# First projection groups of a hybrid decoder step on raw x: the norm's factor and the shift applied to the sums

## The chip, the cores and the metric

The kernel runs on one core of one Trainium2 chip. The time is the device time of one execution in microseconds (us); three executions before the change took 2463.82, 2465.86 and 2465.92, median 2465.86.

The core's engines run side by side, each through its own list of instructions in order: PE multiplies matrices (PEld is its loading of weights), DVE (VectorE), ACT (ScalarE) and POOL (GpSimd) work element by element, SP issues the DMAs here. An instruction waits for the engines whose results or buffers it needs; everything behind it on the same engine waits with it.

## The reference

One decoder layer on 1024 prompt tokens and 8 x 8 sample tokens. What matters here is its start:

```python
mod = jax.nn.silu(c) @ ada_w + ada_b
shift, scale, gate = jnp.split(mod, 3, axis=-1)
h = _rmsnorm(x, norm_g) * (1.0 + scale[:, None]) + shift[:, None]
proj = h @ w_in
```

with `_rmsnorm(x, g) = x * rsqrt(mean(x*x) + EPS) * g`. The prompt has one vector c, each of the 8 sample sequences its own, so that scale and shift have nine columns. The projection's parts then go through windowed attention, a gated MLP and a matrix memory, and an output projection; none of that is touched by the change.

## The kernel before

**Layout.** x is held transposed: 16 tiles (k = 0 to 15) of 128 features by 1088 tokens (1024 of the prompt, 64 samples), worked on in chunks of 384, 384 and 320 tokens (`CH`, line 25). Everything is float32. For the products each value is split into a high part, rounded to the fast matmul format, and a low part, the rest; three matmuls (high by high, high by low, low by high: `products`, lines 249 to 254) make one product. So every tile of the normed and modulated x becomes hH[k] and hL[k], and every weight block becomes wh (rounded by ACT, line 98) and wl (subtracted by POOL, line 99). SP loads the blocks ahead of time into four buffers, and four split blocks exist at a time.

**The start (lines 300 to 595).** In this order:
- SP loads the constants, c, all 16 tiles of x (line 312), then the modulation's weights in pieces of 0.5 MB (lines 326 and 329), four buffers ("ad") at a time, and the first weight blocks.
- As each tile lands, ACT or DVE squares it (lines 387, 389), and PE adds up the squares over the features with a matmul by ones (`token_sums`, line 272). After the sixteenth, `token_rsqrt` (lines 275 to 297) turns the sums, takes the root with three steps of Newton on DVE, and lets PE and ACT spread the result over all partitions: rbc, the norm's factor of each token.
- Tiles are multiplied by rbc (`scaled`, line 398): 0 and 1 by DVE, the others by POOL.
- The modulation comes in groups of two tiles. `ada_half` (tiles 0 and 1, four pieces each) and `ada_group` (two tiles, eight pieces) multiply silu(c) by the pieces in four sets, ACT copies the sums, PE turns them (line 374), DVE reduces them and adds the constants (lines 376, 409 to 411). Then DVE multiplies and shifts the tile (line 420; lines 423 and 424 for the samples), ACT rounds it to hH (line 425), DVE (for four tiles POOL) subtracts to hL (line 431).
- Four column tiles (the v part of the gated MLP) are accumulated meanwhile in four SBUF accumulators acc0 to acc3: for each group g of two tiles there are 12 units (four columns by three chunks) of six matmuls in one of four PSUM buffers, and DVE adds each to its accumulator (line 584). Group 0 is run as two single tiles (lines 542 to 570), groups 1 to 7 in the loop at 574. The table `AT` says after which unit of a group which step of a later modulation group is issued: that hand-written order is the order in each engine's list.
- `gate_column` (lines 625 to 636) follows as the first stage that needs all 16 hH and hL; then come the other columns, which keep PE busy to the end of the kernel.

hH, hL, x and the squares share 33 buffers of one tile each ("slots", line 123).

Of the kernel before, what the change touches and what calls it, by code (L numbers as in the profile page):

```python
# [20 lines left out]
NB = 8  # L21
# [52 lines left out]
class Weights:  # L74
# [16 lines left out]
    def split_to(self, j):  # L91
        while self.ns <= min(j, len(self.jobs) - 1):
            self.dma_to(self.ns)
            n = self.jobs[self.ns][1] * 128
            raw = self.raw.pop(self.ns)
            wh = self.pool.tile([128, 512], FR, tag="wh", name="wh", bufs=4)
            wl = self.pool.tile([128, 512], FR, tag="wl", name="wl", bufs=4)
            self.nc.scalar.copy(wh[:, :n], raw[:, :n])  # L98
            self.nc.gpsimd.tensor_tensor(wl[:, :n], raw[:, :n], wh[:, :n].bitcast(FT), op=OP.subtract)  # L99
            self.parts[self.ns] = (wh, wl)  # L100
            self.ns += 1
# [10 lines left out]
def body(tc, I, O):  # L112
# [162 lines left out]
    def token_rsqrt(ps, n, out, wait):  # L275
# [3 lines left out]
        S.copy(t[64:96, :320], ps[64:96, :320])  # L279
# [23 lines left out]
    ctt = et("ctt")[:, :KT * ND9].rearrange("p (k r) -> p k r", k=KT)  # L303
    SP.dma_start(c9, I["cT"])
    S.activation(ctt, c9, AF.Tanh, scale=0.5)
    V.tensor_scalar(c9, c9, 0.5, None, op0=OP.mult)
    V.scalar_tensor_tensor(c9, ctt, 1.0, c9, op0=OP.add, op1=OP.mult)

    xs = []
    for k in range(KT):  # L310
        x = slot("x")
        SP.dma_start(x, I["xT"][k])
        xs.append(x)
# [21 lines left out]
    def ada_set(ps, s_):  # L335

        ada_dma(used[0] + 4)
# [8 lines left out]
    def ada_half(k):  # L346

        ps = bank("ad")
        for s_ in range(4):
            ada_dma(used[0] + 4)  # L350
# [9 lines left out]
        md01.extend(modulation(k, 1, ada_turn(t)))  # L360
# [18 lines left out]

    ada_dma(4)  # L380
    W.dma_to(1)
    md01 = []
    ps = bank("st")
    for k in range(KT):
# [5 lines left out]
        token_sums(ps, sq, k == 0, k == KT - 1)  # L390
    rbc = s0.tile([128, TOK], FT, tag="big", name="rbc", bufs=5)
    root = token_rsqrt(ps, D, rbc, 1)
    next(root)

    hH, hL = [], []

    def scaled(k, eng):
        eng.tensor_tensor(xs[k], xs[k], rbc, op=OP.mult)
# [15 lines left out]
    def modulate(k, md, t0=0, t1=TOK):  # L414

        x = xs[k]
        if t0 == 0:
            hH.append(slot("hH", FR))
        a = slice(t0, min(t1, NPR))
        V.tensor_scalar(x[:, a], x[:, a], md[:, 1, 0:1], md[:, 0, 0:1], op0=OP.mult, op1=OP.add)  # L420
        if t1 == TOK:
            x3 = x[:, NPR:].rearrange("p (b t) -> p b t", b=NB)
            V.tensor_tensor(x3, x3, md[:, 1, 1:9][:, :, None].to_broadcast([128, NB, NT]), op=OP.mult)
            V.tensor_tensor(x3, x3, md[:, 0, 1:9][:, :, None].to_broadcast([128, NB, NT]), op=OP.add)
        S.copy(hH[k][:, t0:t1], x[:, t0:t1])  # L425

    def modulate_low(k, t0=0, t1=TOK, eng=V):

        if t0 == 0:
            hL.append(slot("hL", FR))  # L430
        eng.tensor_tensor(hL[k][:, t0:t1], xs[k][:, t0:t1], hH[k][:, t0:t1].bitcast(FT), op=OP.subtract)  # L431

    def ada_group(g):

        ps = bank("ad")
        for s_ in range(4):
            ada_set(ps, s_)
            if s_ < 3 and (g == 1 or s_ % 2):
                ada_dma(min(used[0] + 4, 66 if g < 8 else 96))
                yield  # L440
                if g >= 8:
                    yield
        ada_dma(min(used[0] + 4, 66 if g < 8 else 96))
# [66 lines left out]
    for _ in range(2):  # L510
        next(halves[0])
        next(root)
    for _ in root:
        pass
    W.split_to(1)
    for k in range(2):
        scaled(k, V)
    for k in range(2, 6):
        scaled(k, G)
    for _ in range(2):  # L520
        next(halves[0])
    for _ in range(2):
        next(halves[1])
    next(halves[0])
    next(halves[1])
    w0 = [W.get(False), W.get(False)]

    def high(ks, c):
        t0, n = CH[c]
        for k in ks:  # L530
            modulate(k, md01[k], t0, t0 + n)

    def low(ks, c):
        t0, n = CH[c]
        for k in ks:
            modulate_low(k, t0, t0 + n, G if k else V)

    for c in range(3):
        high((0,), c)
        low((0,), c)  # L540

    for k in range(2):
        for c, (t0, n) in enumerate(CH):
            for j in range(NST):
# [3 lines left out]
                products(ps, n, wh[:, o:], wl[:, o:], [(hH[k], hL[k])], t0, True, True)  # L548
# [16 lines left out]
                if k == 1 and u in (6, 8, 10):
                    low((2, 3), (u - 6) // 2)
                if (k, u) in ((0, 10), (1, 5)):
                    W.split_to(2 + k)
        if k == 0:
            W.dma_to(5)  # L570
    AT = [{2: (1,), 4: (1,), 5: (1,), 6: (1,), 7: (1,), 8: (2,)} for _ in range(8)]
    AT[1] = {1: (1,), 4: (1,), 6: (1,), 7: (1,), 8: (1,), 9: (1,), 10: (2,)}
    AT[6] = {1: (1,), 4: (1,), 5: (1,), 7: (1,), 8: (1,)}
    for g in range(1, 8):
        u = 0
        for jj in range(2):
            wh, wl = W.get()
            for jt in range(2):
                j = 2 * jj + jt
                a = slice(256 * jt, 256 * jt + 256)  # L580
                for c, (t0, n) in enumerate(CH):
                    ps = mm.tile([128, 512], FT, tag="mm", name="mm")
                    products(ps, n, wh[:, a], wl[:, a], [(hH[k], hL[k]) for k in (2 * g, 2 * g + 1)], t0, True, True)
                    V.tensor_tensor(accs[j][:, t0:t0 + n], accs[j][:, t0:t0 + n], ps[:, :n], op=OP.add)
                    for d in AT[g].get(u, ()):
                        if g + d < 8:
                            next(groups[g + d])
                    if u in (1, 4) and 2 * g + 4 + u // 4 < KT:
# [1205 lines left out]
```

## Time and profile before

| | us |
|---|---|
| runs (three) | 2463.82, 2465.86, 2465.92 |
| profiled execution | 2462.13 |
| its span, first to last instruction | 2460.1 |
| PE busy | 2419.0 |
| first product of the projection | 47.2 |
| first matmul of the gate column | 198.5 |

A profiled execution is read in views: a page with the busy time of each engine and the span in 40 slices (a digit is the busy share of a slice in tenths); groups of instructions by source line; the chain of waits, followed back from the end; a timeline; and the busy time by stretches. In a row of the timeline stand the start, the time taken, engine, line, operation, what is written and read, and how many instructions were merged; in brackets how long the engine had been idle and who released it.

### The profile page before, as it was taken

How to read it: one execution, taken by the hardware profiler on the slowest of the kernel's cores; microseconds unless marked ns; L12 is line 12 of the kernel's file. 1: busy time of each engine (PE TensorE's matmuls, PEld its weight loads, DVE VectorE, ACT ScalarE, POOL GpSimd, SP SyncE). 2: the span in 40 equal slices, each digit the busy share in tenths (PEclk: the TensorE clock that was granted, in tenths of full speed). 3: DMA queues.
4: the chain of work that ended last, by engine and by line, in shares of the span. 5: the costliest groups of instructions: out<-in, count | busy, mean ns of one | idle time of the engine just before them, and what ended most of it. 6: DMA issues, size and time to landing. Idle time of an engine off the chain costs nothing.

```text
span 2460.1 us, 39820 instructions
## 1 busy us (share of the span) xinstructions
PE 2419.0 (98%) x15879; PEld 2237.5 (91%) x15879; DVE 923.8 (38%) x2489; ACT 746.1 (30%) x1638; POOL 644.3 (26%) x502
## 2 busy tenths in 40 slices
PE   5899999999999999999999999999999999999999
PEld 2677899999999999999999999888989999999898
DVE  5662300323232231323352001333311688887322
ACT  3222221323323232323321111222212566666210
POOL 2431222232322232222221322121211333332321
PEclk8999999999999999999999999999999999999999
DMA  8774621111121112112411524657565855554454
GB/s 289 255 258 158 220 65 44 57 62 57 54 65 58 53 49 73 38 52 71 127 56 59 172 76 171 223 178 265 188 240 187 255 157 165 152 151 139 164 171 141
DMA packets 157081, 332.95 MB, mean 135 GB/s; under 512 B 21770, under 2 KB 76834, under 8 KB 149216
## 3 DMA queue, kind: packets, MB, share of 16 engines
q1 hardware_dynamic: 156896, 330.41, 41.1%
q8 instruction: 125, 2.05, 0.3%
q14 instruction: 60, 0.49, 0.1%
HBM read 284.26 MB, written 54.55 MB: 138 GB/s over the span
## 4 chain that ended last, share of the span: by engine, by line
PE 95%; DMA 2%; DVE 2%; issue 0%; SPq 0%; ACT 0%; POOL 0%; DVEq 0%; POOLq 0%; ACTq 0%
PE mm L252 27%; PE mm L254 26%; PE mm L253 26%; PE pt L1493 2%; PE ad L342 2%; PE os L1300 1%; PE o L1504 1%; PE sq L1250 1%; PE o L1502 1%; DMA ad<-in_adaw 1%; PE s L1452 1%; PE s L1451 1%; DMA x<-in_xT 1%; PE b L942 0%; PE b L974 0%; PE b L982 0%
## 5 line engine op out<-in xcount | busy, mean ns | idle before, releaser
L252 PE MATMUL mm<-hH,wh 128*128 128x384 f32 (+1 forms) x3168 | 1058.5, 334 | 9.3 <-ACT hH L425 8.1
L253 PE MATMUL mm<-hL,wh 128*128 128x384 f32 (+1 forms) x3168 | 1034.8, 327 | 2.6 <-DVE hL L431 2.6
L254 PE MATMUL mm<-hH,wl 128*128 128x384 f32 (+1 forms) x3168 | 1036.0, 327 | 0.0
L99 POOL TENSOR_TENSOR wl<-wraw,wh 128x512 fp32r<-128x512 f32 x344 | 445.7, 1304 | 1545.8 <-ACT wh L98 1433.4
L252 PEld LDWEIGHTS mm<-hH,wh 128*128 128x128 f32 x3168 | 595.9, 188 | 51.3 <-issue 32.1
L253 PEld LDWEIGHTS mm<-hL,wh 128*128 128x128 f32 x3168 | 596.3, 188 | 4.4 <-DVE hL L431 3.6
L254 PEld LDWEIGHTS mm<-hH,wl 128*128 128x128 f32 x3168 | 595.4, 188 | 0.0
L98 ACT CAST wh<-wraw 128x512 fp32r<-128x512 f32 x344 | 200.8, 596 | 409.6 <-PE mm L253 270.9
L252 PE MATMUL mm<-yH,wh 128*128 128x512 f32 (+2 forms) x768 | 261.7, 341 | 0.0
L254 PE MATMUL mm<-yH,wl 128*128 128x512 f32 (+2 forms) x768 | 251.7, 328 | 0.4 <-POOL wl L99 0.4
L253 PE MATMUL mm<-yL,wh 128*128 128x512 f32 (+2 forms) x768 | 251.7, 328 | 0.0
L254 PEld LDWEIGHTS mm<-yH,wl 128*128 128x128 f32 x768 | 144.8, 189 | 11.7 <-POOL wl L99 0.9
L252 PEld LDWEIGHTS mm<-yH,wh 128*128 128x128 f32 x768 | 145.1, 189 | 9.6
L253 PEld LDWEIGHTS mm<-yL,wh 128*128 128x128 f32 x768 | 145.3, 189 | 9.3
L898 DVE SCALAR_TENSOR_TENSOR u<-R,cw,u 128x384 f32<-128x384 f32 (+1 forms) x108 | 62.0, 574 | 213.3 <-ACT u L896 210.8
L1588 DVE SCALAR_TENSOR_TENSOR xo<-mm,gate,xo 128x512 f32<-128x512 f32 (+2 forms) x96 | 54.5, 569 | 117.4 <-PE mm L254 101.8
L1494 ACT CAST pH<-pt 128x512 fp32r<-128x512 f32 (+1 forms) x120 | 65.3, 544 | 63.3 <-PE pt L1493 62.5
L1495 DVE TENSOR_TENSOR pL<-pt,pH 128x512 fp32r<-128x512 f32 (+1 forms) x120 | 74.8, 623 | 11.6 <-ACT pH L1494 11.2
L1463 ACT ACTIVATE P<-P,mx 128x128 f32<-128x128 f32 (+3 forms) x96 | 74.4, 777 | 1.0 <-DVE mx L1460 1.0
L1493 PE MATMUL pt<-cst,P 128*128 128x128 f32 x432 | 66.6, 272 | 0.0
L1454 DVE CUSTOM_DVE_ANT_0 P<-s,btab 128x384 f32<-128x384 f32 (+2 forms) x96 | 54.7, 570 | 30.0 <-PE s L1452 29.1
L1504 PE MATMUL o<-pL,vh 128*64 128x256 f32 x240 | 61.8, 281 | 1.9 <-DVE pL L1495 1.9
(324 smaller groups left out, 2378.8 us busy)
## 6 DMA issues: line engine op xcount, KB each, us to landing
wraw<-in_win SPq DMA_DIRECT2D x264, 256.0 KB
ad<-in_adaw SPq DMA_DIRECT2D x96, 512.0 KB
kv<-in_ck SPq DMA_DIRECT2D x30, 1024.0 KB
kv<-in_cv SPq DMA_DIRECT2D x30, 1024.0 KB
wraw<-in_wout SPq DMA_DIRECT2D x48, 256.0 KB
x<-in_xT SPq DMA_DIRECT2D x16, 544.0 KB
yraw<-yD SPq DMA_DIRECT2D x16, 544.0 KB
xo<-in_xT SPq DMA_DIRECT2D x16, 544.0 KB
```

The source lines that it names most:

```text
L98: self.nc.scalar.copy(wh[:, :n], raw[:, :n])
L99: self.nc.gpsimd.tensor_tensor(wl[:, :n], raw[:, :n], wh[:, :n].bitcast(FT), op=OP.subtract)
L252: T.matmul(ps[:, :n], wh[:, a], rh[:, t0:t0 + n], start=first and i == 0, stop=False)
L253: T.matmul(ps[:, :n], wh[:, a], rl[:, t0:t0 + n], start=False, stop=False)
L254: T.matmul(ps[:, :n], wl[:, a], rh[:, t0:t0 + n], start=False, stop=last and i == len(rows) - 1)
L898: V.scalar_tensor_tensor(u[:, :npr], R[:, j:j + npr], cw[:, m, j:j + 1], u[:, :npr], op0=OP.mult, op1=OP.add)
L1454: V.tensor_tensor_reduce(s[:, k0:k0 + w], ps[:, :w], e["bt"][:, x:x + w], 1.0, mx[:, np_ - 1:np_] if np_ else -3.0e38, op0=OP.add, op1=OP.max,
L1463: S.activation(s[:, :nk], s[:, :nk], AF.Exp, bias=mx[:, 2:3], accum_out=mx[:, 3:4])
L1493: T.transpose(pt[:, o:o + 128], P[r][:, k:k + 128], ident)
L1494: S.copy(pH[:, f:], pt[:, f:])
L1495: at(0, 3, lambda: V.tensor_tensor(pL[:, f:], pt[:, f:], pH[:, f:].bitcast(FT), op=OP.subtract))
L1504: T.matmul(po[0][0:64, :256], e["vh"][:, kb, 0, :], pL[:, c], start=False, stop=(kb == 2 * m + 1), skip_group_check=True)
```

## The change

The products of groups 0 to 2 (`NRAW = 3`, six tiles) are taken of x times (1 + scale), without the norm's factor and without the shift. Since the factor belongs to a token, that is to a column of the accumulator, the sums so far can be multiplied by it once it is known: in group 3 each accumulator is multiplied by rbc ahead of its addition. The shift's part of these groups is a product of its own: `shift_sums` multiplies the split weights by the split shifts of the six tiles (18 columns: nine high, nine low), and the result `ssum` is added in group 3 as well.

The order changes with it:
- SP loads x0, the first weight block, half 0 of the modulation's weights, block 1, x1, half 1; then pieces, x2, x3, blocks; x4, x5; x6 to x15 in one block after group 0. Pieces of groups up to 4 use slots beside the four "ad" buffers, and more are asked for ahead.
- Squares and token sums are spread: tile 0 before the first product, tile 1 after the first tile's products, 2 and 3 after the second's, 4 and 5 in group 1, 6 to 15 in group 2 (table `STAT`); the root is taken at the end of group 2.
- Groups 0 to 3 run chunk by chunk instead of column by column. Tiles 6 and 7 are multiplied by scale and factor in one operation by DVE, and ACT adds the shift while it rounds.
- POOL multiplies tiles 8 to 15 by the factor, and later tiles 0 to 5 (table `SCALED`), from which hH and hL of these six tiles are made anew in groups 5 to 7 (`HIGH`, `LOW`), since the later columns need them.

```diff
+    NRAW = 3
...
-        ada_dma(used[0] + 4)
+        ada_dma(used[0] + (8 if used[0] < 36 else 4))
...
+    xload(0, 1)
+    W.dma_to(0)
     ada_dma(4)
     W.dma_to(1)
+    xload(1, 2)
+    ada_dma(8)
...
+    def raw_high(k, c):
...
+        V.tensor_scalar(x[:, a], x[:, a], md[k][:, 1, 0:1], None, op0=OP.mult)
+        if c == 2:
+            per_batch(x, k, 1, OP.mult)
+        S.copy(rH[k][:, t0:t0 + n], x[:, t0:t0 + n])
...
+        V.tensor_tensor(rL[k][:, a], xs[k][:, a], rH[k][:, a].bitcast(FT), op=OP.subtract)
...
+    def shift_sums(g, w):
...
+        for j in range(NST):
+            wh, wl = w[j // 2]
+            for i in range(2):
...
+                T.matmul(ps[:, 32 * j:32 * j + 18], wh[:, a], s2, start=(i == 0), stop=False, skip_group_check=True)
+                T.matmul(ps[:, 32 * j:32 * j + 18], wl[:, a], s2, start=False, stop=(i == 1), skip_group_check=True)
...
+        if fused:
+            V.scalar_tensor_tensor(x[:, a], x[:, a], md[k][:, 1, 0:1], rbc[:, a], op0=OP.mult, op1=OP.mult)
+        S.activation(hH[k][:, a], x[:, a], AF.Identity, bias=shift(k)[:, 0:1])
...
+    W.split_to(0)
+    sums(0, square(0))
+    for _ in range(5):
         next(halves[0])
...
+    ada_dma(12)
+    xload(2, 4)
+    W.dma_to(3)
+    ada_dma(16)
     W.split_to(1)
...
+    sq2, sq3 = square(2), square(3)
+    shift_sums(0, w0)
+    sums(2, sq2)
+    sums(3, sq3)
+    W.split_to(3)
+    ada_dma(20)
+    xload(4, 6)
+    W.dma_to(5)
+    ada_dma(24)
+    xload(6, KT)
+    W.dma_to(7)
+    for _ in range(3):
+        next(groups[1])
...
+    AT[3] = {1: (0, 1), 3: (1,), 4: (0,), 5: (1,), 7: (1,), 8: (1,), 9: (1,), 10: (1,), 11: (1, 2)}
...
+    STAT = {(1, 5): (4,), (1, 6): (5,), (2, 0): (6, 7), (2, 1): (8,), (2, 2): (9,), (2, 3): (10,), (2, 4): (11,),
+            (2, 5): (12,), (2, 6): (13,), (2, 7): (14,), (2, 8): (15,)}
+    SCALED = {(3, 0): 8, (3, 2): 9, (3, 6): 10, (3, 9): 11, (4, 0): 0, (4, 3): 12, (4, 6): 13, (4, 9): 1,
+              (5, 1): 14, (5, 4): 15, (5, 6): 2, (5, 9): 3, (6, 0): 4, (6, 3): 5}
...
+            if g == NRAW:
+                V.tensor_tensor(acc, acc, rbc[:, t0:t0 + n], op=OP.mult)
             ps = mm.tile([128, 512], FT, tag="mm", name="mm")
+            products(ps, n, wh[:, a], wl[:, a], hh, t0, True, True)
+            if g != NRAW:
+                V.tensor_tensor(acc, acc, ps[:, :n], op=OP.add)
+            else:
+                m = min(n, NPR - t0)
+                V.scalar_tensor_tensor(acc[:, :m], ps[:, :m], ssum[:, j, 0:1], acc[:, :m], op0=OP.add, op1=OP.add)
...
+        if g == 2:
+            next(groups[3])
+            next(groups[3])
+            for _ in range(3):
+                next(root)
+            next(groups[3])
```

More of the change, by code (lines that the diff above doesn't have):

```diff
@@ L359, in ada_half @@
         yield
[L360 removed]
+        md[k] = modulation(k, 1, ada_turn(t))[0]
         yield
@@ L378, in ada_turn, with square @@
         return s
+    xload(0, 1)
+    W.dma_to(0)
     ada_dma(4)
     W.dma_to(1)
-    md01 = []
-    ps = bank("st")
-    for k in range(KT):
+    xload(1, 2)
+    ada_dma(8)
+    md = [None] * KT
+    ssum = s0.tile([128, NST, ND9], FT, name="ssum")
+    shifts = s0.tile([128, 2 * NRAW, ND9], FT, name="shifts")
+    sts = bank("st")
+    def square(k):
         sq = slot("sq")
@@ L389, in body, with sums, scaled @@
             S.activation(sq, xs[k], AF.Square)
-        token_sums(ps, sq, k == 0, k == KT - 1)
+        return sq
+    def sums(k, sq):
+        token_sums(sts, sq, k == 0, k == KT - 1)
     rbc = s0.tile([128, TOK], FT, tag="big", name="rbc", bufs=5)
[L392 to L398, printed above, removed]
+    root = token_rsqrt(sts, D, rbc, 1)
+    hH, hL = [None] * KT, [None] * KT
+    rH, rL, sh = {}, {}, {}
+    def scaled(k):
+        G.tensor_tensor(xs[k], xs[k], rbc, op=OP.mult)
     def modulation(k, nk, ads):
@@ new lines, in raw_low, with shift_parts @@
+    def raw_low(k, c):
+        t0, n = CH[c]
+        if c == 0:
+            rL[k] = slot("rL", FR)
+        a = slice(t0, t0 + n)
+        V.tensor_tensor(rL[k][:, a], xs[k][:, a], rH[k][:, a].bitcast(FT), op=OP.subtract)
+    def shift_parts(k):
+        V.tensor_copy(shifts[:, k], md[k][:, 0])
+        sh[k] = s0.tile([128, 2, ND9], FR, tag="sh", name="sh", bufs=2)
+        S.copy(sh[k][:, 0], md[k][:, 0])
+        V.tensor_tensor(sh[k][:, 1], md[k][:, 0], sh[k][:, 0].bitcast(FT), op=OP.subtract)
@@ L509, in body @@
     halves = [ada_half(k) for k in range(2)]
-    for _ in range(2):
+    W.split_to(0)
+    sums(0, square(0))
+    for _ in range(5):
         next(halves[0])
-        next(root)
-    for _ in root:
-        pass
+    ada_dma(12)
+    xload(2, 4)
+    W.dma_to(3)
+    ada_dma(16)
     W.split_to(1)
[L516 to L525, printed above, removed]
-    w0 = [W.get(False), W.get(False)]
[L528 to L540, printed above, removed]
+    for c in range(3):
+        raw_high(0, c)
+        raw_low(0, c)
+    shift_parts(0)
+    w0 = [W.get(False), W.get(False)]
     for k in range(2):
@@ L565, in body @@
[L565 to L568, printed above, removed]
-        if k == 0:
[L570 to L573, printed above, removed]
-    for g in range(1, 8):
[L575 to L588, printed above, removed]
-                        scaled(2 * g + 4 + u // 4, G)
-                    if g == 6 and u == 11:
-                        gate_weights()
-                    age()
-                    u += 1
-                if g == 7:
-                    later(lambda j=j: SP.dma_start(vbD[j], accs[j]), 2)
@@ new lines, in body @@
+                if k == 1 and u in (3, 7):
+                    next(groups[1])
+        if k == 0:
+            sums(1, square(1))
+            next(halves[1])
+            for c in range(3):
+                raw_high(1, c)
+                raw_low(1, c)
+            shift_parts(1)
+    sq2, sq3 = square(2), square(3)
[9 more added lines that the diff above has]
+    W.dma_to(7)
```

205 lines of the change are left out of this document (152 added, 53 removed).

## The prediction

> **What bounds the kernel now.** I began with the page: share of busy time, then the slices.
>
> ```profile
> PE 2419.0 (98%) x15879; PEld 2237.5 (91%) x15879; DVE 923.8 (38%) x2489; ACT 746.1 (30%) x1638; POOL 644.3 (26%) x502
> PE   5899999999999999999999999999999999999999
> ```
>
> PE is busy 98% of the span; only the first two slices (61.5 us each) show a gap. So time can be won at the start alone, and whatever is added to PE later is paid in full. The view by stretches of time cuts the start at the first product, at the first product of group 1 and round one steady group; the source view of L632 shows where the stage ends (the gate column follows the last product). After the stretch come its length and the busy time of PE, PE's weight loads, DVE, ACT and POOL, then clock, DMA share and GB/s.
>
> ```profile
> 0.00:47.20 47.20, 23.24 (x167) 6.48 (x167) 22.29 (x29) 14.68 (x19) 10.53 (x10) 0.94 0.95 332
> 47.20:76.40 29.20, 24.11 (x118) 15.85 (x119) 17.48 (x34) 10.95 (x26) 11.20 (x9) 0.80 0.62 208
> 76.40:101.20 24.80, 21.53 (x128) 13.75 (x127) 14.95 (x31) 5.34 (x9) 13.39 (x11) 1.00 0.59 198
> ...
> 119.40:135.90 16.50, 16.50 (x110) 13.18 (x109) 11.96 (x25) 3.90 (x6) 8.50 (x5) 1.00 0.79 286
> ...
> L632 PE MATMUL mm<-hH,ifw x48: 309/337/338, 198.5 to 214.1; 128*64 128x384 f32 x32, 128*64 128x320 f32 x16
> ```
>
> Until 47.2 us DMA is 95% busy and PE multiplies nothing for the projection. A steady group is all PE (16.50 of 16.50), with DVE at 12.0 and POOL at 8.5. The stage runs from 47.2 to 198.5. The chain of waits says what holds the first product:
>
> ```profile
> 7.47 9.79 DMA x<-in_xT
> 17.28 10.86 DMA x<-in_xT
> 28.17 1.30 DVE sq L387
> ...
> 39.67 0.64 PE ad L353 x8
> 40.31 0.38 PE at L374 x2
> 40.72 0.24 DVE ads L376
> ...
> 41.67 2.34 DVE md L411
> 44.04 2.60 DVE x L420
> 46.66 0.52 ACT hH L425
> ```
>
> All 16 tiles of x come first, then the statistics, then the modulation's weights, then the first tile.
>
> **What the change removes: the wait for 15 tiles.** Now x0, one weight block and four pieces of the modulation's weights are enough. Their landings, from the timeline:
>
> ```profile
> 7.79 1.11 ACT L389 ACTIVATE sq<-x 128x1088 f32<-128x1088 f32 x1 [1.12 <-DMA x<-in_xT]
> 28.17 1.29 DVE L387 TENSOR_TENSOR sq<-x 128x1088 f32<-128x1088 f32 x1 [1.45 <-DMA x<-in_xT]
> 39.67 0.16 PEld L353 LDWEIGHTS ad<-ad,csp 128*32 128x32 f32 x8 [1.11 <-DMA ad<-in_adaw]
> 41.14 0.16 PEld L353 LDWEIGHTS ad<-ad,csp 128*32 128x32 f32 x8 [0.70 <-DMA ad<-in_adaw]
> ```
>
> x0 lands at 7.8; an x tile takes (28.17 - 7.79)/15 = 1.36 us, a weight block of half the size 0.65, a piece 1.4 (41.14 - 39.67 = 1.47 at most). 7.8 + 0.65 + 4 x 1.4 = 14.1. Behind the last piece stand one set (0.64), copy and turn (0.8), reduction and three small operations (0.7), multiplication (0.4) and rounding (0.52), with handovers 3.5: 17.6. In the chain above this tail took 47.2 - 39.67 = 7.5, because POOL was multiplying tiles (below); now one POOL operation of 1.3, the split of block 1, can fall into it. I take 0.9 of it: **first product at 18.5**, 28.7 earlier. Bounds 17.6 and 21 (two POOL operations, one late piece).
>
> **What it adds to PE.** Rows of the timeline, PE:
>
> ```profile
> 15.93 0.84 PE L272 MATMUL st<-sq,cst 128*32 128x384 f32 x6 [0.68 <-DVE sq L387]
> ...
> 34.48 1.86 PE L295 MATMUL rb<-cst,rs 128*128 128x128 f32 x9 [1.75 <-DVE rs L225]
> ...
> 131.10 1.92 PE L342 MATMUL ad<-ad,csp 128*32 128x512 f32 x16
> ...
> 133.58 0.33 PE L252 MATMUL mm<-hH,wh 128*128 128x384 f32 x1
> 133.75 0.33 PE L253 MATMUL mm<-hL,wh 128*128 128x384 f32 x1
> ...
> 135.14 0.31 PE L252 MATMUL mm<-hH,wh 128*128 128x320 f32 x1
> 135.28 0.30 PE L253 MATMUL mm<-hL,wh 128*128 128x320 f32 x1
> ...
> 143.67 0.60 PE L374 MATMUL at<-cst,at 128*128 128x128 f32 x4
> ```
>
> Products start every 0.174 us (384 columns) and 0.146 (320): a group has 48 and 24, 11.9 us. This is unchanged, and so are the modulation's sets (two in 1.85, 3.7 a group) and turns (0.4). New on PE after the first product:
> - Token sums of 15 tiles, 0.8 each (0.84 with its tail): 12.0. Formerly they lay under the loading. Those of tile 1 fall into a wait: 11.2.
> - The root: nine broadcasts 1.86 and four turns 0.8: 2.7.
> - Half 1: two more sets than before (four 0.64 against two): 1.3.
> - The shifts' products: 48 matmuls of 18 columns, which no row shows. Upper end 0.207 each (1.86/9): 9.9; lower end next to nothing. I take 0.11, from the four turns in 0.44 (0.60 with the tail): 5.3.
>
> Together 20.5, so **28.7 - 20.5 = 8.2 us** remain if the waits are as long as before. Before, they are 151.3 (47.2 to 198.5) less the work: 8 x 11.9 products, 7 x 3.7 sets, 1.3 for half 1, 3 for turns, 125.4; so 26: 11.5 before group 1 and 8.8 in it (below), the rest spread over groups 2 to 7, mostly for pieces.
>
> **What it does to the waits.** Cold clock and handovers of the two single tiles: 11.5 of the 29.2 us before group 1 were waits (less 11.9, 1.3, 3.7 and 0.8). Now: cold clock 2.5, tile 0 to 1 (set, copy, turn, modulation, rounding, less the sums) 2.1, DVE late with tile 1's splitting 1.4, the same chain ahead of group 1 3.2, together 9.2. Group 1 waited 8.8 (24.8 less 16) for pieces behind busy queues; now the shifts' products cover most of that chain: 0.5. Ahead of group 3, root and modulation: 2.2. On SP, the request for group 2's first four pieces waits until group 1's first two sets have freed their buffers, at about 36. Behind it stand four more pieces, blocks 4 to 7 and x tiles 4 to 15, and group 3's pieces behind all of them: 8 x 1.4 + 4 x 0.65 + 12 x 1.36 = 30, so the last tile lands at 66. Group 2, which takes its squares, begins at about 72, so I charge nothing; if it is late, each tile costs 1.4. Behind the stage only the gates' pieces are asked for a step later; three of the four buffers remain full, no charge. Stores and split blocks keep their order.
>
> New is **group 3**, where DVE does what nobody did before. Rows of DVE:
>
> ```profile
> 165.09 0.55 DVE L584 TENSOR_TENSOR acc<-acc,mm 128x384 f32<-128x384 f32 x1
> 165.55 1.29 DVE L431 TENSOR_TENSOR hL<-x,hH 128x1088 fp32r<-128x1088 f32 x1
> ...
> 169.40 1.80 DVE L584 TENSOR_TENSOR acc<-acc,mm 128x320 f32<-128x320 f32 x4
> ...
> 179.85 0.81 DVE L420 TENSOR_SCALAR x<-x,md 128x1024 f32<-128x1024 f32 x1
> 180.58 0.22 DVE L423 TENSOR_TENSOR x<-x,md 128x64 f32<-128x64 f32 x1
> 180.83 0.23 DVE L424 TENSOR_TENSOR x<-x,md 128x64 f32<-128x64 f32 x1
> ```
>
> Per unit of 384: accumulator times factor (0.46 from start to start) and a sum of three terms that must wait for it (0.57): 1.03, eight times 8.2. Per unit of 320, with the samples' two small additions: 0.4 + 0.43 + 0.17 + 0.25 = 1.25, four times 5.0. Tiles 6 and 7, chunks 1 and 2, fused multiply and low part: 2.2 + 3.1. Tiles 8 and 9: reduction and modulation 0.8, multiplication 2 x 1.25, low part 2 x 1.2: 5.7. Sum 24.2, and the last low part, which group 4 needs, is issued last. PE has 11.9 + 3.7 + 0.9 + 0.4 = 16.9, and with four PSUM buffers it can't run further ahead: **7.8 us** of waiting with the first unit's. The fused three-operand forms and ACT's rounding with a bias have no row; the operations of equal size (0.49 to 0.57 on DVE, 0.52 on ACT) bound them within 1 us in all. Groups 5 to 7 get the low parts of tiles 0 to 5 (1.5 each) on DVE's 12 of 16.5: 2.5 for backlog.
>
> POOL multiplies tiles 8 to 11 and splits two blocks in the same group. What that does to DVE:
>
> ```profile
> L99 POOL TENSOR_TENSOR wl<-wraw,wh x344: 731/1293/3066, 37.4 to 2439.3; 128x512 fp32r<-128x512 f32 x164, 128x256 fp32r<-128x256 f32 x8
> ...
> 41.50 10.23 POOL L398 TENSOR_TENSOR x<-x,rbc 128x1088 f32<-128x1088 f32 x4
> 41.67 2.33 DVE L411 SCALAR_TENSOR_TENSOR md<-md,cst 128x9 f32<-128x9 f32 x1
> 44.04 2.59 DVE L420 TENSOR_SCALAR x<-x,md 128x384 f32<-128x384 f32 x1
> ...
> 167.03 3.60 POOL L99 TENSOR_TENSOR wl<-wraw,wh 128x512 fp32r<-128x512 f32 x2 [8.65 <-PE ad L342]
> 167.22 2.25 DVE L431 TENSOR_TENSOR hL<-x,hH 128x1088 fp32r<-128x1088 f32 x1
> ```
>
> At 41.67 an operation of nine elements took 2.33 us, one POOL operation long. In a steady group, with 8.5 us of POOL, DVE lost only 2.25 - 1.29 = 1.0. The cost in group 3 lies between nothing and POOL's whole time, 4 x 2.6 + 2 x 1.3 = 13. I take 3, nearest to the steady groups (1.0 in 8.5 us of POOL, with only the last rows' overlap), since half of DVE's operations read PSUM, and the additions show 0.55 beside POOL as without it.
>
> Waits after: 9.2 + 0.5 + 2.2 + 7.8 + 2.5 + 3 = 25.2 against 26. **Sum:** 18.5 + 125.4 + 20.5 + 25.2 = 189.6, and 198.5 - 189.6 = 8.9; I say 8. The profiled execution took 2462.1 (span 2460.1 and 2.0 around it); the median shown is 2465.9, 3.7 longer. Taken off the median: **2458**.
>
> **The rivals.**
> (1) *POOL holds DVE throughout.* POOL needs only the factor's broadcast, so tiles 8 and 9 start before group 3's small modulation operations, as at 41.67: two POOL operations delay the first product by 4.2, the other four cost DVE 5.6. The same happens to the turn in group 4 (three POOL operations, 4) and in group 6 (2). That is 15.8 in place of 3: 12.8 more, 2471, slower. It decides from about 3 + 8 = 11 us. For it: the rows at 41.67 and 44.04; against it: the steady groups.
> The Trainium skill, "SBUF — State Buffer", section "Who interferes with whom", says that a VectorE instruction with two SBUF inputs and a GpSimd one that reads SBUF exclude each other for a whole instruction. The row at 41.67 agrees; by that rule alone this rival would be the forecast.
> (2) *DVE keeps up.* Operations overlap or PE's waits cover them: the 7.8 and the 3 go, 2447. For it: DVE is at 38% over the span; against it: the sum of 24.2.
> (3) *The start gains less.* The pieces queue behind tiles, first product at 21, shifts' products at 0.207: 2.5 + 4.6, or 2465, within the noise; with late x tiles in group 2 (four, 5.6) 2471.
> The cold clock (0.80 in the second stretch) comes back in each case.
>
> **How the numbers follow.** Forecast 0.42, rival 1 0.27, rival 2 0.17, rival 3 0.14. 0.2% is 4.9 us, about what a measurement of this kernel can tell from no change. Of the forecast 0.33 lies beyond that and 0.09 within; rival 2 is faster; rival 1 is 0.20 slower and 0.07 within (held in part); rival 3 is 0.07 within and 0.07 slower. Faster 0.50, same 0.23, slower 0.27. The forecast's own range is 2452 to 2464; the range goes to rivals 1 and 2: 2446 to 2472.
>
> **What would show it.** First product (L252's successor) between 17.6 and 21; x6 to x15 landed before 70; the shifts' matmuls 2 us a group; group 3 at 24 to 28 us with PE waiting for DVE's last low part; DVE's small modulation operations at 0.2 us there, not 2.3. The gate column should start at 190. I am wrong if group 3 begins later than 105, or lasts over 32.

## The result, and the profile after

The changed kernel is **slower**, by 1.6%: 2503.99 us, median of four runs (2499.93 to 2505.32), against 2464.84 (four runs, 2461.82 to 2465.92); the ratio is 1.0158, 95% interval 1.014 to 1.0176. The prediction of 2458 and its range, up to 2472, missed. The profiled execution has a span of 2500.9 us against 2460.1.

First the page of the kernel after: the first row of the busy times and PE's row of the 40 slices.

```profile
PE 2438.3 (97%) x15927; PEld 2252.5 (90%) x15927; DVE 958.5 (38%) x2568; ACT 755.4 (30%) x1664; POOL 635.1 (25%) x493
PE   7868999999999999999999999999999999999999
```

The gap of the start is smaller in the first slice (7 for 5) and a new one stands in the third (125 to 188 us): 6 where there was a 9. So a new gap opened in the stage that the early start should have shortened. The view by stretches shows where. The cuts are the first product, the first product of group 2, of group 3, the start of group 4, and the first matmul of the gate column. For group 4 the cut before is its first product; after, it is the fifth (with tile 9's low part), since PE stalls in front of that one. Columns as in the prediction. Before:

```profile
0.00:47.22 47.22, 23.24 (x167) 6.48 (x167) 22.31 (x30) 14.68 (x19) 10.55 (x10) 0.94 0.95 331
47.22:100.99 53.77, 45.44 (x242) 29.39 (x243) 32.20 (x64) 16.28 (x35) 24.35 (x18) 0.89 0.61 203
100.99:119.45 18.46, 17.81 (x110) 13.11 (x109) 12.99 (x25) 3.90 (x6) 9.21 (x5) 1.00 0.82 296
119.45:136.01 16.56, 16.56 (x110) 13.24 (x109) 12.02 (x25) 3.90 (x6) 8.56 (x5) 1.00 0.79 287
136.01:198.54 62.53, 61.88 (x383) 51.08 (x382) 44.01 (x87) 12.83 (x20) 22.53 (x12) 1.00 0.66 236
```

After:

```profile
0.00:19.18 19.18, 5.82 (x41) 2.55 (x41) 2.45 (x9) 4.63 (x7) 3.26 (x7) 1.00 0.92 296
19.18:73.83 54.65, 48.77 (x312) 34.72 (x312) 29.59 (x79) 17.07 (x40) 6.08 (x4) 0.97 0.96 365
73.83:112.14 38.31, 31.17 (x198) 19.47 (x198) 26.11 (x56) 11.30 (x22) 8.48 (x4) 0.90 0.49 180
112.14:154.47 42.33, 25.91 (x121) 17.62 (x121) 36.62 (x62) 7.26 (x14) 14.62 (x7) 0.74 0.34 112
154.47:237.02 82.55, 70.84 (x385) 53.93 (x386) 65.17 (x102) 20.35 (x32) 34.90 (x15) 0.91 0.49 169
```

Read the first number behind each stretch, its length. The start gains 28.0 us (47.22 to 19.18), and 27.2 of them are left at group 2 (the stretch takes 54.65 against 53.77). Then group 2 takes 19.9 us more, group 3 with the stall behind it 25.8 more, groups 4 to 7 20.0 more. In group 3 DVE is busy for 36.62 of 42.33 us, PE for 25.91, at a granted clock of 0.74. The gate column starts 38.5 us late (237.02 against 198.54); the remaining 2.3 of the span's 40.8 us come behind it.

The chain of waits in front of group 3 (start, time, what) is the first look at the cause:

```profile
103.85 1.13 PE rb L302 x9
104.98 0.45 PE at L386 x4
105.45 0.32 DVE ads L388
105.80 2.45 DVE md L433
108.37 2.35 DVE md L435
110.82 0.63 DVE x L497
```

Two operations on 18 elements (lines 433 and 435) take 2.4 us each. The timeline shows what ran beside them, and the same in the middle and at the end of group 3:

```profile
105.74 4.93 POOL L422 TENSOR_TENSOR x<-x,rbc 128x1088 f32<-128x1088 f32 x2 [12.62 <-ACT rbc L303]
...
129.57 5.10 POOL L422 TENSOR_TENSOR x<-x,rbc 128x1088 f32<-128x1088 f32 x2
129.81 2.49 DVE L514 TENSOR_TENSOR hL<-x,hH 128x64 fp32r<-128x64 f32 x1
132.22 2.85 DVE L704 TENSOR_TENSOR acc<-acc,rbc 128x384 f32<-128x384 f32 x1
...
148.11 5.16 POOL L422 TENSOR_TENSOR x<-x,rbc 128x1088 f32<-128x1088 f32 x2
148.60 0.48 DVE L711 SCALAR_TENSOR_TENSOR acc<-mm,ssum,acc 128x256 f32<-128x256 f32 x1
...
149.25 1.67 DVE L715 TENSOR_TENSOR acc<-acc,ssum 128x64 f32<-128x64 f32 x1
150.84 3.58 DVE L527 TENSOR_TENSOR hL<-x,hH 128x1088 fp32r<-128x1088 f32 x1
154.47 0.69 PE L260 MATMUL mm<-hL,wh 128*128 128x384 f32 x1 [6.07 <-DVE hL L527]
```

Where POOL multiplies a tile by rbc (line 422, about 2.5 us each), a DVE operation on SBUF tiles beside it lasts until POOL is done, or as long as it takes by itself behind that, whatever its size. Between two multiplications a small one can slip through (0.17 us at 108.17). An operation that reads a product from PSUM (`mm`) is not held: 256 columns took 0.48 us at 148.60, and right behind it 64 columns of `acc` and `ssum`, both in SBUF, took 1.67. PE waits for DVE at the end (6.07 us, the bracket in the last row).

### The profile page after: what moved, and what is told of

Same layout as the page of the kernel before. It is cut to its first block, busy times and chain, and to the rows that moved or that the text cites. A ratio compares the mean times of both kernels' runs of the same rounds, so it can differ in the third digit from the quotient of the medians.

```text
span 2500.9 us, 40003 instructions
## 1 busy us (share of the span) xinstructions
PE 2438.3 (97%) x15927; PEld 2252.5 (90%) x15927; DVE 958.5 (38%) x2568; ACT 755.4 (30%) x1664; POOL 635.1 (25%) x493
## 4 chain that ended last, share of the span: by engine, by line
PE 92%; DVE 4%; DMA 2%; issue 1%; ACT 0%; SPq 0%; POOL 0%; DVEq 0%; ACTq 0%; POOLq 0%
PE mm L259 26%; PE mm L260 25%; PE mm L261 25%; PE pt L1645 2%; PE sq L1402 1%; DMA ad<-in_adaw 1%; PE o L1656 1%; PE os L1452 1%; PE o L1654 1%; PE ad L355 1%; PE s L1604 1%; PE s L1603 1%; DVE hL L527 1%; DMA wraw<-in_win 1%; PE b L1094 0%
## 5 line engine op out<-in xcount | busy, mean ns | idle before, releaser
L259 PE MATMUL mm<-hH,wh 128*128 128x384 f32 (+1 forms) x3096 | 1037.3, 335 | 18.4 <-DVE acc L708 7.9
L260 PE MATMUL mm<-hL,wh 128*128 128x384 f32 (+1 forms) x3096 | 1014.6, 328 | 16.4 <-DVE hL L527 13.3
L261 PE MATMUL mm<-hH,wl 128*128 128x384 f32 (+1 forms) x3096 | 1015.1, 328 | 0.0
L259 PEld LDWEIGHTS mm<-hH,wh 128*128 128x128 f32 x3096 | 584.2, 189 | 62.4 <-issue 34.1
L260 PEld LDWEIGHTS mm<-hL,wh 128*128 128x128 f32 x3096 | 584.8, 189 | 19.6 <-DVE hL L527 15.3
L261 PEld LDWEIGHTS mm<-hH,wl 128*128 128x128 f32 x3096 | 584.1, 189 | 0.0
L260 PEld LDWEIGHTS mm<-yL,wh 128*128 128x128 f32 x768 | 145.3, 189 | 9.3
L1606 DVE CUSTOM_DVE_ANT_0 P<-s,btab 128x384 f32<-128x384 f32 (+2 forms) x96 | 54.7, 570 | 32.1 <-PE s L1604 31.2
```

The source lines that it names most:

```text
L259: T.matmul(ps[:, :n], wh[:, a], rh[:, t0:t0 + n], start=first and i == 0, stop=False)
L260: T.matmul(ps[:, :n], wh[:, a], rl[:, t0:t0 + n], start=False, stop=False)
L261: T.matmul(ps[:, :n], wl[:, a], rh[:, t0:t0 + n], start=False, stop=last and i == len(rows) - 1)
L1606: V.tensor_tensor_reduce(s[:, k0:k0 + w], ps[:, :w], e["bt"][:, x:x + w], 1.0, mx[:, np_ - 1:np_] if np_ else -3.0e38, op0=OP.add, op1=OP.max,
```

## The experiments

Theory **A**: POOL's 14 multiplications by rbc hold DVE back. Rivals: **A'**, DVE and ACT wait for what POOL makes; **B**, weight block 8 comes late; **C**, DVE has too much work of its own. (POOL's multiplications also stand ahead of its own splits of weight blocks. But on the page of the kernel after, the products with the low parts of weights, line 261, have 0.0 us of idle time in front of them, so PE never waited for those.) The table has the starts (us) from the views by source line and the chains, then the time and that of the kernel before on the same chip. The experiments' times are one run each; the kernels timed in rounds stand further down, with their intervals. Single executions scatter: the seven kernels without a POOL multiplication ahead of group 3 (a1, a3, d1, b3, e1, f1, f2) do the same work up to there and reach it at 109.7 to 112.9 us. A difference of less than about 3 us between two rows says little.

| kernel | first product | group 3 | group 4 | gate column | time | before beside it |
|---|---|---|---|---|---|---|
| before | 47.2 | 119.5 | 136.0 | 198.5 | | |
| after | 19.2 | 112.1 | 154.5 | 237.0 | 2503.99 | 2464.84 |
| a1, POOL's multiplications left out | 18.3 | 109.7 | 140.9 | 211.0 | 2476.39 | 2466.14 |
| a2, blocks 8, 9 requested early | 19.1 | 114.7 | 152.4 | 235.3 | 2502.12 | 2466.14 |
| a3, tiles 8 to 15 fused on DVE | 19.0 | 110.2 | 145.3 | 232.2 | 2498.90 | 2466.14 |
| a4, sums' factor left out | 19.4 | 112.2 | 145.3 | 227.4 | 2494.89 | 2466.14 |
| b1, POOL writes to scratch | 19.1 | 114.7 | 153.9 | 236.1 | 2504.89 | 2468.80 |
| d1, multiplications on DVE | 19.2 | 110.4 | 145.2 | 218.5 | 2485.51 | 2468.80 |
| b3, a3 without remaking | 19.2 | 112.7 | 145.6 | 221.1 | 2488.27 | 2468.80 |
| e1, a1 and a4 | 18.7 | 112.1 | 137.5 | 206.8 | 2472.78 | 2463.92 |
| f1, a1 without remaking | 19.0 | 110.0 | 141.6 | 209.2 | 2477.34 | 2469.23 |
| f2, a1, a4 and no remaking | 19.2 | 112.9 | 138.4 | 204.9 | 2471.74 | 2469.23 |

**a1: no multiplication on POOL.** Tiles 8 to 15, and 0 to 5 for the later columns, stay without the factor.

```diff
-            if (g, u) in SCALED:
-                scaled(SCALED[g, u])
```

> POOL's fourteen multiplications of x tiles by the norm's factor are left out (tiles 8 to 15 and 0 to 5 stay unscaled); everything else as in the changed kernel, whose gate column starts at 237.0 us. Theory A (a POOL operation holds DVE's two-input operations for its whole length): DVE's stretched rows in groups 3 to 7 (2.45 and 2.34 for 18 elements, 2.49, 2.85, 3.58, 2.27, 2.39, 3.14, 2.99, 2.60, 2.43 and their like) shrink to their plain lengths, 25 to 30 us in all, so the gate column starts at 207 to 213 and the time falls by as much. Theory B (blocks 8 and 9 requested too late): the 6.5 us of waiting for block 8 stay and the gate column starts above 230. Theory C (DVE's own new work in group 3): 232 to 237.

26.0 of the 38.5 us are gone. The stretches, cut as above from group 2's first product on, and the same two small operations in the timeline:

```profile
75.35:109.73 34.38, 31.61 (x197) 18.36 (x197) 21.58 (x56) 11.39 (x22) 3.55 (x2) 0.95 0.51 183
109.73:140.88 31.15, 22.45 (x120) 15.24 (x121) 27.78 (x62) 7.39 (x14) 5.16 (x3) 0.83 0.46 153
140.88:211.01 70.13, 67.94 (x385) 53.06 (x386) 52.80 (x102) 20.39 (x32) 10.93 (x7) 0.93 0.56 199
```

```profile
107.82 0.18 DVE L433 TENSOR_TENSOR md<-ads,cst 128x18 f32<-128x18 f32 x1
...
108.12 0.18 DVE L435 SCALAR_TENSOR_TENSOR md<-md,cst 128x18 f32<-128x18 f32 x1
```

2.45 and 2.34 us became 0.18. DVE's count of instructions is the same in each stretch (56, 62, 102), but its busy time falls by 4.5, 8.8 and 12.4 us: 25.7, nearly all of the 26.0 that the gate column gains. POOL's own busy time falls by 38.4 (4.9, 9.5, 24.0). So a held DVE shows as *busy*, and lost 0.67 us for each us that POOL multiplied. PE's wait in front of group 3 shows the same without the scatter of the start: 6.6 to 6.8 us in the four kernels with the multiplications there (after, a2, a4, b1), 2.3 in the seven without.

**a2: blocks 8 and 9 requested early.** In the changed kernel, the timeline of SP (start, time taken, what it issued) has these two rows one after the other:

```profile
63.52 55.85 SPq L342 DMA_DIRECT2D ad<-in_adaw  x18
119.46 1.69 SPq L87 DMA_DIRECT2D wraw<-in_win  x3
```

The request for block 8 stood behind modulation pieces that waited for buffers, and ACT waited for it until 126.02.

```diff
                 W.split_to(2 * g + 2 + (u - 5) // 3)
+                if g == 2:
+                    W.dma_to(8 + (u - 5) // 3)
```

> Weight blocks 8 and 9 are requested in group 2, ahead of the modulation's pieces of group 4, not in group 3. Theory B: ACT no longer stands still from 119 to 126 waiting for block 8 with the rounding of tiles 6 and 7 behind it, and the gate column starts at 229 to 231 in place of 237.0. Theory A: POOL's splits and multiplications only come earlier and hold DVE the same; 233 to 236. Theory C: 234 to 237.

ACT's rounding of block 8 moved from 126.02 to 121.50, the gate column by 1.7 us, which is within the scatter (this execution reached group 3 2.6 us later). B is out as a main cause: theory B had the gate column at 229 to 231, and it came at 235.3.

**a3: tiles 8 to 15 take the factor in one DVE operation with the scale.** POOL keeps six of the 14.

```diff
-                high_scaled(k)
+                high(k, fused=True)
...
-                low_scaled(k)
+                low(k)
...
-            if (g, u) in SCALED:
+            if (g, u) in SCALED and SCALED[g, u] < 8:
```

> Tiles 8 to 15 take scale and factor in one DVE operation and the shift in ACT's rounding, as tiles 6 and 7 do; POOL multiplies only tiles 0 to 5. DVE's count rises by about 0.4 us a tile, POOL loses eight operations of 2.5. Theory A: group 3, where POOL then has only the two splits, loses its stretched rows (4.5 ahead of its first product, 5 at chunk 2, 5 at the end), groups 4 to 6 about half of theirs: gate column at 212 to 220. Theory C: DVE is the bound by its own count, 237 to 241. Theory B: 235 to 238.

A miss: 4.8 us instead of 17 or more. Group 4 starts 9.2 us earlier, but groups 4 to 7 take 86.9 (232.17 - 145.30) in place of 82.6. Fusing isn't free: per tile the operation of 1024 columns takes 1.28 us with two tensor inputs where the scale alone took 0.81, and two more of 64 columns come on top (0.22 and 0.21), 0.9 in all, where 0.4 had been expected, on an engine that is late. And the other six multiplications still run there.

**a4: no factor on the sums.** The 12 DVE multiplications of the accumulators in group 3 are left out.

```diff
-            if g == NRAW:
-                V.tensor_tensor(acc, acc, rbc[:, t0:t0 + n], op=OP.mult)
```

> The twelve multiplications of the accumulators by the norm's factor in group 3 are left out (the first three groups' sums stay without it). Theory C: DVE's 12 x 0.5 us and the waits behind them go from group 3, gate column at 228 to 231. Theory A: the POOL operations hold the next two-input operation instead; 233 to 236. Theory B: 235 to 237.

9.6 us, a little beyond theory C's range. The 12 operations by themselves are 6.3 (0.55 and 0.48 us each); two of them had been held beside POOL (2.85 and 1.56 us in the kernel after), which makes up the rest, though no run takes the two apart. DVE's own work counts too, then.

**b1: POOL computes for nobody.** Same reads, same length, result into a spare tile.

```diff
-        G.tensor_tensor(xs[k], xs[k], rbc, op=OP.mult)
+        if not junk:
+            junk.append(slot("junk"))
+        G.tensor_tensor(junk[0], xs[k], rbc, op=OP.mult)
```

> The 14 multiplications of x by rbc on POOL stay, same size and place, but write to a scratch tile (one of the 33 slots), so that nothing waits for their result; later tiles are modulated without their factor. Theory A (POOL's reading holds up DVE, whoever needs the result): all of the loss stays, the gate column begins at 233 to 239 (after 237.0, without the multiplications 211.0) and the operations of 18 elements in group 3 still take 2.3 us; time 2498 to 2505. Theory A' (DVE and ACT wait for what POOL makes): the loss goes as it did without the multiplications, gate column at 209 to 215, time 2474 to 2481.

The whole loss stays (gate column 236.1), and the two small operations (three lines further down here) are as long as ever:

```profile
108.27 2.45 DVE L436 TENSOR_TENSOR md<-ads,cst 128x18 f32<-128x18 f32 x1
...
110.84 2.43 DVE L438 SCALAR_TENSOR_TENSOR md<-md,cst 128x18 f32<-128x18 f32 x1
```

Nothing waits for the scratch tile, so A' falls: it is POOL's running, not its result.

**d1: the same multiplications on DVE.**

```diff
-        G.tensor_tensor(xs[k], xs[k], rbc, op=OP.mult)
+        V.tensor_tensor(xs[k], xs[k], rbc, op=OP.mult)
```

> The same 14 multiplications, on DVE and not on POOL, at the same places of the order. DVE gets 14 x 1.28 us (the 1088-column operation of two inputs with POOL quiet) = 18 us more work of its own. Theory A: the operations of 18 elements in group 3 fall to 0.2 us, what POOL cost (26 us) goes and 8 to 18 us come back as DVE's own work: gate column at 219 to 229, time 2482 to 2495. Theory C (DVE simply has too much to do, POOL is not the cause): 18 us more on the engine that binds, gate column at 237 to 255, time 2504 or more.

18.5 us *faster* than the changed kernel, with more work on the engine that binds. The last two stretches:

```profile
110.37:145.16 34.79, 24.16 (x120) 15.73 (x121) 31.97 (x66) 7.58 (x14) 4.42 (x3) 0.79 0.41 137
145.16:218.52 73.36, 67.16 (x384) 50.81 (x385) 62.97 (x112) 20.24 (x32) 12.06 (x7) 0.96 0.56 193
```

Against a1, DVE is busy 4.2 and 10.2 us longer for the 14 operations; being held by POOL cost it 25.7.

**b3: a3, and no multiplication left for POOL.** Tiles 0 to 5 are not made anew for the later columns (left out).

```diff
-                high(HIGH[g, u])
...
-                low(LOW[g, u])
+                hH[LOW[g, u]], hL[LOW[g, u]] = rH[LOW[g, u]], rL[LOW[g, u]]
```

> No multiplication on POOL at all: tiles 8 to 15 take the factor in DVE's one operation with two inputs, and tiles 0 to 5 are not made anew for the later columns (they stay without factor and shift there, which this kernel leaves out). What is left of the change up to the gate column is the early start, the added PE work of 20.5 us and DVE's load in group 3. Theory A with DVE's load in group 3 as the rest: group 3 as without the multiplications (about 24 us and a stall of 7 to 11 ahead of group 4), groups 5 to 7 at 16 to 18 us each, gate column at 205 to 212, time 2468 to 2476. If making tiles 0 to 5 anew is the larger part of what remains: gate column at 198 to 205, time 2462 to 2469. If groups 5 to 7 stay at 19 us or more without either, something else binds them.

A miss: 221.1, later than both ranges and later than a1 by 10 us. This run mixes two edits; f1 below has the second alone. From group 3 on b3 takes 9.2 us longer than f1 (108.4 against 99.2), and that is the fused form of eight tiles: 0.9 each by the operations' own times are 7.2, the rest is not placed.

**e1: a1 and a4 together.**

> The changed kernel without the 14 multiplications on POOL and without DVE's 12 multiplications of the sums by rbc in group 3 (sums of the first three groups and later tiles stay without factor). Theory: without POOL's hold, group 3 with the stall behind it (31.1 us) is DVE's own work (27.8 us busy); 6.4 us less of it (12 x 0.53) bring the first product with group 4's tiles from 140.9 to 133.5 to 136, gate column at 203 to 206 (after 211.0), time 2466 to 2471. Rival (PE's sets, the clock or weight block 8 set that stretch): no more than 2 us gained, gate column at 209 to 211, time 2474 to 2477.

The stretch of group 3 with its stall:

```profile
112.14:137.48 25.34, 21.39 (x120) 14.99 (x120) 20.72 (x50) 7.38 (x14) 4.01 (x3) 0.90 0.57 189
```

31.15 became 25.34, 5.8 of the 6.4 us left out; the gate column is at 206.8, a little past the range because this execution reached group 3 2.4 us later. So without POOL's multiplications, what lengthens group 3 is mostly DVE's own work.

**f1 and f2: no remaking of tiles 0 to 5**, on top of a1 and of e1 (tiles 0 to 5 as in b3).

> Without POOL's 14 multiplications and without making tiles 0 to 5 anew for the later columns (both left out, nothing put in their place). With the multiplications alone left out, groups 4 to 7 took 70.1 us against 62.5 before. Theory (remaking keeps DVE busy, 13 to 15 us of a group's 15 to 18, as the busy times of groups 5 to 7 say): groups 5, 6 and 7 fall to before's 17.2, 15.4 and 13.0, 4 us in all, group 4 stays at 20 for its low clock; gate column at 206 to 208 (after 211.0), time 2470 to 2473. Rival (what remains there is PE's own, after a pause with a low clock): gate column at 210 to 212, time 2475 to 2478.

> The same, and without DVE's 12 multiplications of the sums by rbc in group 3. If the three costs are separate: 206.8 (the two others left out) less 4: gate column at 202 to 204, time 2465 to 2469; what is left against before's 198.5 is then the added PE work less the early start. If they cover each other: 205 to 207, time 2468 to 2472.

Both came out between the theories: 209.2 and 204.9. f1's stretches of groups 4 and 7 say why:

```profile
141.63:162.16 20.53, 20.53 (x113) 14.07 (x113) 10.48 (x22) 3.89 (x6) 2.57 (x2) 0.84 0.57 193
...
196.24:209.15 12.91, 12.33 (x75) 11.80 (x74) 9.89 (x16) 0.63 (x1) 3.80 (x3) 1.00 0.47 170
```

Group 7 is back at before's 13.0, but group 4 stays at 20.5 though PE never waits in it: its clock is 0.84 after the pause in front of it, where before it was 1.00 and 16.9 us (136.01 to 152.94). Up to 147 us its products of 384 columns start every 0.32 us, from 149 on every 0.17. Remaking costs 2.6 us in groups 4 to 7 (70.13 to 67.52; 2.8 between e1 and f2), the clock after the pause about 3.6.

**c2, c1, c3, c4: the same hold in the kernel before.** Four DVE operations stand beside POOL's first four multiplications there, two ahead of its first product and two right behind it. c2 issues the multiplications later:

```diff
-    for k in range(2, 6):
-        scaled(k, G)
...
+                if (k, u) in ((0, 0), (0, 2), (1, 0), (1, 2)):
+                    scaled(2 + 2 * k + u // 2, G)
```

> The kernel before, with POOL's first four multiplications of x by rbc (10.2 us, right ahead of the first product) issued during the first products instead. In the kernel before they run beside four DVE operations of the path to the first product, which take 2.33, 2.59, 2.18 and 2.65 us. Theory A (a POOL operation holds back a DVE operation that starts beside it): these take 0.2 and 0.4 to 0.6 us, the first product begins at 42.6 to 43.6 instead of 47.2, and the time falls by 2 to 4.5 us (ratio 0.998 to 0.999) unless the same hold costs it again in the first products' modulations. Theory without the hold (those operations are slow for a reason of their own, or the start waits for weights): first product at 46.5 to 47.5, ratio 0.9995 to 1.0005.

Neither: the first product stayed at 48.0, and the ratio is 1.0007 (0.9998 to 1.0016). The timeline of c2 shows why:

```profile
42.23 4.91 POOL L398 TENSOR_TENSOR x<-x,rbc 128x1088 f32<-128x1088 f32 x2
...
42.40 2.33 DVE L411 SCALAR_TENSOR_TENSOR md<-md,cst 128x9 f32<-128x9 f32 x1
44.77 2.59 DVE L420 TENSOR_SCALAR x<-x,md 128x384 f32<-128x384 f32 x1
47.93 0.56 DVE L431 TENSOR_TENSOR hL<-x,hH 128x384 fp32r<-128x384 f32 x1 [0.58 <-ACT hH L425]
48.41 0.48 DVE L420 TENSOR_SCALAR x<-x,md 128x384 f32<-128x384 f32 x1
...
70.16 4.99 POOL L398 TENSOR_TENSOR x<-x,rbc 128x1088 f32<-128x1088 f32 x2
...
71.00 1.70 DVE L409 TENSOR_TENSOR md<-ads,cst 128x18 f32<-128x18 f32 x1
```

POOL ran the first two at once, since issuing an instruction later in the text doesn't make an idle engine wait. The two operations whose neighbours did move became short (2.18 to 0.56, 2.65 to 0.48); and where the moved pair landed, at 70.2, it held the next group's modulation. The mechanism showed itself again, twice, and the edit was worth nothing (gate column at 203.8, in an execution 2.5 us above the median of this kernel).

c1 takes POOL out of it: scale and factor in one DVE operation for all tiles, ACT adds the shift, and DVE also makes the low parts that POOL made.

```diff
-        V.tensor_scalar(x[:, a], x[:, a], md[:, 1, 0:1], md[:, 0, 0:1], op0=OP.mult, op1=OP.add)
+        V.scalar_tensor_tensor(x[:, a], x[:, a], md[:, 1, 0:1], rbc[:, a], op0=OP.mult, op1=OP.mult)
+        S.activation(hH[k][:, a], x[:, a], AF.Identity, bias=md[:, 0, 0:1])
...
-    for _ in range(2):
+    for _ in range(3):
         next(halves[0])
-    for _ in range(2):
+    for _ in range(3):
         next(halves[1])
-    next(halves[0])
-    next(halves[1])
```

> The kernel before, without any separate multiplication by rbc: DVE takes scale and factor in one operation, ACT adds the shift while it rounds, DVE's remainder adds it again; the first half's modulation is turned ahead of the second half's sets. POOL then only makes the low parts of weights. Theory A: first product at 41.5 to 43.5 (before 47.2), groups 3 to 6 at 15.4 to 17 us each as before (DVE goes from 12 of 16.6 us to 14), time lower by 3 to 7 us (ratio 0.997 to 0.999). Rival: DVE's added operations of 64 columns and the longer operations with two inputs make it late in groups 2 to 7, which gives the gain back: gate column at 197 or later, ratio 0.9995 or more.

First product at 42.2, as expected, but the rival came true: groups 3 to 5 take 18.7 us each in place of 16.6 to 17.2 (DVE busy 14.4 of them, bunched behind the turn of the next tiles, and the chain runs through it), the gate column starts at 206.3, the ratio is 1.0032 (1.0019 to 1.0045). c3 fuses tiles 0 to 5 alone:

```diff
+        if k >= 6:
+            eng.tensor_tensor(xs[k], xs[k], rbc, op=OP.mult)
```

> The kernel before with DVE's operation of scale and factor for tiles 0 to 5 alone; from tile 6 on POOL multiplies by rbc as before, so that DVE has in groups 3 to 6 the 12 us of 16.6 that it had. Theory (the start gains because POOL is quiet there, groups 2 to 6 lost it to DVE's longer operations where all tiles were fused): first product at 42 to 43, group 2 at 94 to 97 (before 101.0), groups 3 to 6 at 16.5 to 17.3 us each as before, gate column at 191 to 195 (before 198.5), ratio 0.997 to 0.999. Rival (the modulation pieces and weight blocks, requested only as buffers come free, set the pace of groups 1 and 2, so that an earlier start is waited away): gate column at 197 or later, ratio 0.9995 to 1.0005.

First product at 41.5, group 2 at 94.7, but the gate column at 200.3, as the rival had it; ratio 0.9994 (0.9985 to 1.0003), no difference. c3's chain shows two takers:

```profile
77.80 6.42 DMA ad<-in_adaw
...
96.36 2.97 DVE hL L445
99.33 2.46 DVE hL L448
```

A modulation piece that is requested only when a buffer comes free, and POOL's multiplications of tiles 6 and 7, which now meet tile 5's low parts. c4 adds an early request for weight blocks 2 and 3 to c3:

```diff
+    W.dma_to(3)
     w0 = [W.get(False), W.get(False)]
```

> The same, and weight blocks 2 and 3 requested ahead of the first products. In the kernel before (62.5 to 67.8 us) and with all tiles fused (54.9 to 61.0 us) the chain waits 5.3 and 6.1 us for block 2, whose request stands on SP behind modulation pieces that wait for buffers, with ACT's copies of a set's sums behind its rounding. Theory (a request stuck behind waiting ones, as with block 8 in the changed kernel): that wait goes, second products and group 1 start 3 to 6 us earlier than without this edit, gate column at 187 to 192, ratio 0.995 to 0.998. Rival (the pieces are the limit: 0.5 MB of blocks ahead of them delay each by 1.5 to 2.8 us and group 1 begins no earlier): ratio within 0.0008 of the kernel without this edit.

Ratio 0.9981 (0.9972 to 0.999), 2459.32 us against 2464.17: the only version that beats both kernels, by 0.2%. That lies between the theory (0.995 to 0.998) and the rival (within 0.0008 of c3). Its profiled execution (span 2461.9) has the wait for block 2 gone and group 1 1.4 us earlier than c3's, yet the gate column at 198.7, level with before; so that trace does not place the gain, and where it lies stays open.

## Why the prediction was wrong, step by step

- **The start, 18.5.** Right: 19.2.
- **The added PE work.** The piece without a row was right, 16 products of shifts in 1.8 us (43.12 to 44.90), 0.11 each. The tiles of x were asked for by 59.7, and no square waited. Not priced: that PE's work is longer at a lower clock (0.90 in group 2 and 0.95 in a1's, 1.00 before). Even without POOL's multiplications group 3 began only at 109.7 to 112.9; the prediction had named 105 as its limit.
- **The step that failed:** "The cost in group 3 lies between nothing and POOL's whole time, 4 x 2.6 + 2 x 1.3 = 13. I take 3". Leaving the multiplications out shortened that group with its stall by 11.2 us, the end of group 2 by 3.9 and groups 4 to 7 by 12.4. The argument for 3 was the steady groups, where DVE lost 1.0 us in 8.5 of POOL. But there POOL's multiplications meet hardly anything that is held. In group 3 of the kernel before:

```profile
119.86 5.00 POOL L398 TENSOR_TENSOR x<-x,rbc 128x1088 f32<-128x1088 f32 x2
...
120.72 0.56 DVE L584 TENSOR_TENSOR acc<-acc,mm 128x384 f32<-128x384 f32 x1 [0.25 <-PE mm L254]
```

  In these 5.0 us DVE runs additions from PSUM alone, at their usual length. The prediction saw that such additions pass; what it missed is that group 3 is full of operations on SBUF tiles (the sums times rbc, the low parts, the modulation), on a DVE busy for 36.6 of 42.3 us. The rows at 41.67 and 44.04 us, where such operations waited beside POOL, were the ones to go by.
- **Rival 1 had the mechanism and its rule.** The Trainium skill, "SBUF — State Buffer", section "Who interferes with whom", says that a VectorE instruction with two SBUF inputs and a GpSimd one that reads SBUF exclude each other. The runs agree: held at 2.45 us beside POOL, 0.18 without, 2.45 with POOL's result unused. Held was also an operation with a single input tile, the multiplication and shift of 384 columns (the prediction's row at 44.04): 2.59 us beside POOL in c2, 0.48 without. But the rival's price was 15.8 (12.8 more than the forecast's 3) against 26.0 measured. Of its parts, the 4.2 ahead of group 3 was right (2.45 + 2.34 less 2 x 0.18 is 4.4, and so is 6.7 of waiting less 2.3); 5.6 in group 3 stood against 11.2, and 6 in groups 4 and 6 against 12.4 in groups 4 to 7, where POOL's multiplications go on to group 6 while DVE makes tiles 0 to 5 anew.
- **Group 3's own work, 24.2 us of DVE and 7.8 of waiting.** Too small: with POOL's multiplications gone, DVE is busy 27.8 us and the group takes 31.2 with the stall, 14.6 more than before. e1 shows that DVE sets it: 6.4 us of its work less, 5.8 us gained.
- **"2.5 for backlog" in groups 5 to 7** is near the 2.6 of f1 for the remaking. What was missing is the low clock after the stall ahead of group 4, about 3.6 us.
- **Block 8's request** stuck on SP was not seen; a2 shows 1.7 us for it, no more than the scatter.

Together: the gate column came 47.4 us behind the predicted 189.6 (237.0). POOL's multiplications cost 26.0 (a1) where 3 was allowed, so the failed step is 23 of the 47; the rest lies in the late start of group 3, in its own work and behind its stall, as above. Without them, the sums' factor is another 4.2 (e1), and the remaking 1.9 (f2 against e1). The order of leaving out matters: with the sums' factor gone first, it is 9.6 (a4), and POOL's multiplications 20.6 (e1 against a4).

With all three gone (f2) the gate column is at 204.9, still 6.4 us later than before, though the start is 28.0 earlier. The 34.4 us between lie in three places: 21.5 from the first product to group 3 (93.7 against 72.2), where the added PE work falls; 8.9 in group 3 (25.5 against 16.6), where DVE is still busy for 20.7; 4.0 in groups 4 to 7 (66.5 against 62.5). What part of each is the low clock was not taken apart. So even without these three costs no run shows a gain; f2's one time, 2471.74 against 2469.23, is too close to tell from none.

## What to carry to other kernels

Before an operation is given to an idle POOL, look at what DVE does at that moment. If it has operations on SBUF tiles waiting, each us of a multiplication on POOL cost DVE 0.67 us here, and doing it on DVE (1.3 us instead of 2.5) was 18.5 us cheaper over 14 operations. Price contention from a row in which the same kind of operation stood beside POOL, not from a stretch in which DVE read PSUM. And an early start pays only as far as the engine that gets the postponed work has room: here 28 us won at the front met an engine that could not take the added work in the groups behind.

## What the runs showed of the hardware

- Beside a POOL multiplication of two SBUF tiles, DVE operations on SBUF tiles waited (18 elements 2.45 us, 0.18 without; a multiplication and shift of one tile, 384 columns, 2.59 and 0.48), and operations with an input in PSUM did not (0.48 us for 256 columns, 0.56 for 384).
- A held DVE instruction counts as busy for its whole wait: the same 62 instructions in group 3 show 36.62 us beside POOL's multiplications and 27.78 without. High busy time of DVE is no proof of much work; the mean time of small operations is (18 elements: 2.45 us or 0.18).
- A pause cost twice. After the stall ahead of group 4 in f1, PE's clock was low and a group without any wait took 20.5 us in place of 16.9 (clock 0.84 and 1.00), so that about 3.6 us came on top of the pause.
